# Other order of the seven products of a two-by-two block product in a decoder layer's feed-forward stages

## The chip, the cores and the metric

One core of one Trainium2 chip runs the whole kernel. The metric is the device time of one execution in microseconds (us). Its engines are TensorE (matmuls), VectorE, ScalarE and GpSimd (POOL) for element-wise work, and SyncE (SP), whose queue issues the weight loads. Each engine takes the instructions of its own queue in order; semaphores order them between engines.

## The reference

One layer of a decoder for 512 prompt tokens and 8 x 4 sample tokens, 544 columns in all; x is 544 x 1024, the hidden size of the feed-forward stages is 2816:

```
x = x + 0.5 * swiglu(rmsnorm(x, g1), wg1, wu1, wd1)      # feed-forward 1
h = rmsnorm(x, g2) @ w_in ; conv group and sparse attention group -> y
x = x + y @ w_out                                        # the middle stage
x = x + 0.5 * swiglu(rmsnorm(x, g3), wg2, wu2, wd2)      # feed-forward 2
swiglu(x, wg, wu, wd) = (silu(x @ wg) * (x @ wu)) @ wd
```

Everything is float32. The change touches only x @ wg and x @ wu of the two feed-forward stages.

## The kernel before

Activations lie transposed: 128 channels on the partitions, 544 token columns beside them, 8 chunks of channels. To keep float32 precision with TensorE's faster format, each operand is split into a high part (`whi`, rounded by ScalarE) and a low part (`wlo`, the rest, by VectorE), and a product is three matmuls: high by high, high by low, low by high.

A feed-forward stage runs over blocks of hidden chunks of 128 (`BLOCKS`, line 30): (0, 6), (6, 14), (14, 22) in the first, (0, 8), (8, 16), (16, 22) in the second. A block computes its hidden chunks and then multiplies them by their rows of `wd` (`Y`, lines 487 to 511), a stretch of 384 matmuls or less in which VectorE has little to do. The first six chunks of stage 1 and the first four of stage 2 are computed plainly (`G` and `U` at L195). All others go in pairs of chunks through `hidden` (line 415): 17 pairs, each a unit G (gate) and a unit U (up), 34 units in five stretches of 4, 4, 2, 4 and 3 pairs.

A unit (`unit`, line 362) is a two-by-two block product by Strassen's scheme in Winograd's form. The left side is the weight, in four quarters: a11 and a12 (halves of the inner dimension, first chunk of the pair), a21 and a22 (second chunk). The right side is the normed activation, halved by inner dimension and by columns. Seven products take the place of eight: three on raw quarters (a11, a12, a22) and four on sums s1 = a21 + a22, s2 = s1 - a11, s3 = a11 - a21, s4 = a12 - s2. Each is 12 matmuls of 272 columns (4 chunks by 3 split terms), so a unit is 84 matmuls. Counting from 0, the order of the products before is a11, s1, s2, a12, s3, s4, a22.

`factors` (line 268) prepares the left side of one unit. Two DMAs bring (a11, a12) and (a21, a22) into staging tiles `wst` (three in one pool and a fourth, `wst4`, so that two units' weights are staged). `parts` (line 282) splits: (a11, a12) together at line 293, 128 x 1024, from `wst`; (s1, s2) at line 298 and (s3, s4) at line 299, 128 x 1024 each, from `s`; a22 alone at line 300, 128 x 512, from `wst`. The sums are four POOL instructions (line 297) in tiles s12 and s34 of one buffer each. Split weights have few buffers: three slots `whi0` to `whi2`, one for each of the three pairs, and one pair of tiles for a22. So the split of a pair for the next unit can start only when both products of that pair in the running unit are done.

`right` (line 311) prepares the seven right-hand sides once a stage, in two halves of k0. Its splits are numbered 0 to 6 in the order in which they are written, and `self.rights` lists them for `unit`; the last is that of a22.

Products leave PSUM by ScalarE copies m1 and m5 (lines 375, 376) and VectorE additions into z, a tile of seven parts (lines 377, 379, 380, 381, 385), after which come silu (line 418), the product of gate and up (line 421) and the split of the hidden chunks hh, hl (lines 483, 484). PSUM tiles: f has two banks, s and t one each, w is two tiles of two banks.

The order on each engine's queue is not the order of the code: it is fixed before the run by the scheduler behind `TileContext`, which knows the dependencies and the buffers and gives each instruction its place. `unit` names the products in one order, and `factors` returns the left sides, and `self.rights` the right sides, in the same order.

Of the kernel before, what the change touches and what calls it, by code (L numbers as in the profile page):

```python
# [14 lines left out]
AF = mybir.ActivationFunctionType  # L15
# [6 lines left out]
HT = T // 2  # L22
# [99 lines left out]
class Trunk:  # L122
# [63 lines left out]
    def wmm(self, unit, parts, act, cuts=HALVES, which=(0, 1)):  # L186

        wh, wl = parts
        ah, al = act
        n = wh.shape[1]  # L190
        for k in range(n):
            for j, (a, b) in enumerate(((wh, ah), (wh, al), (wl, ah))):
                for i in which:
                    c0, c1 = cuts[i]
                    self.nc.tensor.matmul(unit[:, i, :c1 - c0], a[:, k, :], b[:, k, c0:c1],  # L195
                                          start=k == 0 and j == 0, stop=k == n - 1 and j == 2)
# [71 lines left out]
    def factors(self, srcs, nk):  # L268


        nc = self.nc
        st = []
        for load in srcs:
            self.staged += 1
            pool, tag = (self.fp, "wst4") if self.staged % 4 == 0 else (self.sp, "wst")
            t = pool.tile([128, 2 * nk * 128], F32, name="wst", tag=tag, bufs=1 if pool is self.fp else WB).rearrange("p (h k m) -> p h k m", h=2, k=nk)
            for dst, src in load(t):
                nc.sync.dma_start(dst, src)
            st.append(t)
        (a11, a12), (a21, a22) = [(t[:, 0], t[:, 1]) for t in st]  # L280

        def parts(src, n):
            if n == 1:
                ts = [self.fp.tile([128, nk * 128], F32R, name=nm, tag=nm + "4", bufs=1) for nm in ("whi", "wlo")]
            else:
                slot, self.slot = self.slot, (self.slot + 1) % 3
                ts = [self.sp.tile([128, n * nk * 128], F32R, name=nm, tag=f"{nm}{slot}", bufs=1) for nm in ("whi", "wlo")]
            hi, lo = (t.rearrange("p (h k m) -> p h k m", h=n, k=nk) for t in ts)
            nc.scalar.activation(hi, src, AF.Copy)  # L289
            nc.vector.tensor_sub(lo, src, hi.bitcast(F32))  # L290
            return [(hi[:, h], lo[:, h]) for h in range(n)]

        p11, p12 = parts(st[0], 2)
        s12, s34 = (self.fp.tile([128, 2, nk, 128], F32, name=n, tag=n, bufs=SB) for n in ("s12", "s34"))
        for dst, a, b, op in ((s12[:, 0], a21, a22, ALU.add), (s12[:, 1], s12[:, 0], a11, ALU.subtract),
                              (s34[:, 0], a11, a21, ALU.subtract), (s34[:, 1], a12, s12[:, 1], ALU.subtract)):
            nc.gpsimd.tensor_tensor(dst, a, b, op=op)  # L297
        p1, p2 = parts(s12, 2)
        p3, p4 = parts(s34, 2)
        p22, = parts(st[1][:, 1:2], 1)  # L300
        return p11, p1, p2, p12, p3, p4, p22

    def parts_of(self, u, k, hh, hl):

# [6 lines left out]
    def right(self, scale, place):  # L311


        nc, fp, n = self.nc, self.fp, KC // 2
        V, P = nc.vector, nc.gpsimd
        x3 = [fp.tile([128, 3, n, HT], F32R, name=nm, tag=nm, bufs=1) for nm in ("x3h", "x3l")]
        x4 = [self.xp.tile([128, 4, n, HT], F32R, name=nm, tag=nm, bufs=1) for nm in ("xh", "xl")]
        places = [(x3, 0), (x3, 1), (x3, 2), (x4, 0), (x4, 2), (x4, 1), (x4, 3)]
        self.rights = [[a[:, j] for a in t] for t, j in places]
        for k0 in range(0, n, 2):  # L320
            v, t3 = place(k0)

            def row(r):
                for k in range(2):
                    c, dst = r * n + k0 + k, v[r][:, k].rearrange("p c n -> p (c n)")
                    if r == 0 or self.alone:
                        V.scalar_tensor_tensor(dst, self.x[:, c, :], scale[:, c:c + 1], self.R, op0=ALU.mult, op1=ALU.mult)
                    else:
                        nc.scalar.activation(dst, self.x[:, c, :], AF.Copy, scale=scale[:, c:c + 1])
                        P.tensor_tensor(dst, dst, self.R, op=ALU.mult)  # L330

            def split(i, src):
                t, j = places[i]
                hi, lo = (a[:, j, k0:k0 + 2] for a in t)
                nc.scalar.activation(hi, src, AF.Copy)
                V.tensor_sub(lo, src, hi.bitcast(F32))

            (b11, b12), (b21, b22) = [[v[r][:, :, c] for c in range(2)] for r in range(2)]
            less = (V if self.alone else P).tensor_tensor
            row(0)  # L340
            split(0, b11)
            yield
            row(1)
            yield
            less(t3, b22, b12, op=ALU.subtract)
            V.tensor_sub(b12, b12, b11)
            split(1, b12)
            yield
            less(b11, b22, b12, op=ALU.subtract)
            split(2, b11)  # L350
            yield
            split(3, b21)
            yield
            split(4, t3)
            yield
            less(b21, b21, b11, op=ALU.subtract)
            split(5, b22)
            yield
            split(6, b21)
            yield  # L360

    def unit(self, name, left, right, nk, z):

        nc = self.nc
        V, EV = nc.vector, getattr(nc, EVICT)
        m1, m5 = (self.fp.tile([128, HT], F32, name=n, tag=n, bufs=ZB) for n in ("m1", "m5"))

        def product(n, out):
            (wh, wl), (bh, bl) = left[n], right[n]
            for k in range(nk):  # L370
                for j, (w, b) in enumerate(((wh, bh), (wh, bl), (wl, bh))):
                    nc.tensor.matmul(out, w[:, k, :], b[:, k, :], start=k == 0 and j == 0, stop=k == nk - 1 and j == 2)  # L372
            return out

        nc.scalar.activation(m1, product(0, self.funit(name)[:, :HT]), AF.Copy)  # L375
        nc.scalar.activation(m5, product(1, self.funit(name)[:, :HT]), AF.Copy)
        V.tensor_add(z[:, 0], product(2, self.sunit(name)[:, :HT]), m1)
        p = product(3, self.tunit(name)[:, :HT])
        V.tensor_add(z[:, 3], p, m1)
        V.tensor_add(z[:, 2], product(4, self.funit(name)[:, :HT]), z[:, 0])  # L380
        EV.tensor_tensor(z[:, 1::5], z[:, 0:3:2], m5[:, None, :].to_broadcast([128, 2, HT]), op=ALU.add)
        w = self.wunit(name)
        product(5, w[:, 0, :HT])
        product(6, w[:, 1, :HT])
        V.tensor_add(z[:, 4:6], w[:, :, :HT], z[:, 1:3])

    def ffn(self, wg, wu, wd, scale, done, late=False):
# [155 lines left out]
    def begin_units(self):  # L543

        nc, tc, i = self.nc, self.tc, self.i
        with tc.high_priority(offset=FIRST):
# [74 lines left out]
            def mms(unit, w, hf, order="01234567" * 2):  # L621

                c0, c1 = TILES[hf]
                seen = set()
                for n, ch in enumerate(order):
                    k = int(ch)
                    _, wh, wl = (x[:, k % x.shape[1]] for x in w[k * len(w) // KC])
                    todo = [(wl, self.xh)] if k in seen else [(wh, self.xh), (wh, self.xl)]
                    seen.add(k)
                    for a, b in todo:  # L630
                        pin(nc.tensor.matmul(unit[:, hf, :c1 - c0], a, b[:, k, c0:c1], start=n == 0 and b is self.xh, stop=n == 2 * KC - 1))
# [1068 lines left out]
```

## Time and profile before

| what | us |
|---|---|
| time, median of 3 runs | 1253.94 (1253.44 to 1253.94) |
| the profiled execution, its own time | 1253.65 |
| its span in the profile | 1251.9 |
| TensorE busy | 1192.6 (95%) |
| VectorE busy | 858.7 (69%) |
| ScalarE busy | 544.2 (43%) |
| POOL busy | 446.3 (36%) |
| L372, the units' matmuls | 2856 of the 9216 matmuls |

A busy share is a mean over stages with different limits. PE is TensorE's matmul row, DVE VectorE, ACT ScalarE. Matmuls are pipelined: each lasts 0.29 us in the profile, and the next starts 0.125 us after it.

### The profile page before, as it was taken

How to read it: one execution, taken by the hardware profiler on the slowest of the kernel's cores; microseconds unless marked ns; L12 is line 12 of the kernel's file. 1: busy time of each engine (PE TensorE's matmuls, PEld its weight loads, DVE VectorE, ACT ScalarE, POOL GpSimd, SP SyncE). 2: the span in 40 equal slices, each digit the busy share in tenths (PEclk: the TensorE clock that was granted, in tenths of full speed). 3: DMA queues.
4: the chain of work that ended last, by engine and by line, in shares of the span. 5: the costliest groups of instructions: out<-in, count | busy, mean ns of one | idle time of the engine just before them, and what ended most of it. 6: DMA issues, size and time to landing. Idle time of an engine off the chain costs nothing.

```text
span 1251.9 us, 22739 instructions
## 1 busy us (share of the span) xinstructions
PE 1192.6 (95%) x9216; PEld 1070.5 (86%) x9221; DVE 858.7 (69%) x1433; ACT 544.2 (43%) x830; POOL 446.3 (36%) x465
## 2 busy tenths in 40 slices
PE   8999999999999998899979999989989999999998
PEld 7999989999998747775667545779989999999998
DVE  6449998359965208999999753246997379845972
ACT  6224544134444455465534546335444134423432
POOL 2202651145302536665423222221650255204500
PEclk9999999999999998999998999999999999999999
DMA  8523224223331562245214544544223312432332
GB/s 239 140 68 105 73 86 134 86 69 90 94 104 59 168 199 85 65 139 169 66 58 142 163 135 140 164 136 135 77 60 110 110 55 86 123 93 71 95 86 75
DMA packets 184364, 136.08 MB, mean 109 GB/s; under 512 B 5706, under 2 KB 172434, under 8 KB 184260
## 3 DMA queue, kind: packets, MB, share of 16 engines
q1 hardware_dynamic: 171700, 91.62, 25.3%
q0 software_dynamic: 11904, 42.26, 10.5%
q8 instruction: 72, 1.18, 0.4%
q10 hardware_dynamic: 656, 0.76, 0.2%
q14 instruction: 32, 0.26, 0.1%
HBM read 131.66 MB, written 2.96 MB: 108 GB/s over the span
## 4 chain that ended last, share of the span: by engine, by line
PE 67%; DVE 22%; issue 5%; DMA 3%; ACT 2%; POOL 1%; DVEq 0%; ACTq 0%; POOLq 0%
PE Y L195 21%; PE U L372 10%; PE G L372 6%; DVE wlo L290 5%; PE Yo L134 3%; PE lg L134 3%; PE U L195 3%; PE nat L134 3%; PE KTp L138 3%; PE G L195 2%; DVE flip L1010 2%; DMA ckn<-in_cache_k,ik 1%; PE ssc L134 1%; DVE u L421 1%; PE O L134 1%
## 5 line engine op out<-in xcount | busy, mean ns | idle before, releaser
L297 POOL TENSOR_TENSOR s<-wst 128x512 f32<-128x512 f32 x68 | 98.2, 1448 | 363.7 <-DMA wst<-in_ffn_w_gate 209.0
L170 ACT ACTIVATE whi<-wst 128x1024 fp32r<-128x1024 f32 (+3 forms) x105 | 99.9, 957 | 203.9 <-PE Y L195 72.5
L195 PE MATMUL Y<-hl,whi 128*128 128x272 f32 (+2 forms) x704 | 147.8, 288 | 0.0
L195 PE MATMUL Y<-hh,whi 128*128 128x272 f32 (+2 forms) x704 | 147.6, 289 | 0.0
L195 PE MATMUL Y<-hh,wlo 128*128 128x272 f32 (+2 forms) x704 | 147.5, 288 | 0.0
L175 DVE TENSOR_TENSOR wlo<-wst,whi 128x1024 fp32r<-128x1024 f32 (+3 forms) x88 | 99.8, 1134 | 21.3 <-ACT whi L170 19.7
L195 PEld LDWEIGHTS Y<-hl,whi 128*128 128x128 f32 x704 | 111.5, 188 | 0.0
L195 PEld LDWEIGHTS Y<-hh,wlo 128*128 128x128 f32 x704 | 111.3, 188 | 0.0
L195 PEld LDWEIGHTS Y<-hh,whi 128*128 128x128 f32 x704 | 110.8, 188 | 0.0
L290 DVE TENSOR_TENSOR wlo<-wst,whi 128x1024 fp32r<-128x1024 f32 (+1 forms) x68 | 96.3, 1416 | 15.4 <-ACT whi L289 15.0
L509 DVE SCALAR_TENSOR_TENSOR x<-Y,x 128x544 f32<-128x544 f32 x46 | 33.2, 723 | 105.0 <-PE Y L195 105.0
L289 ACT ACTIVATE whi<-s 128x1024 fp32r<-128x1024 f32 x68 | 71.8, 1056 | 70.9 <-PE Y L195 29.8
L290 DVE TENSOR_TENSOR wlo<-s,whi 128x1024 fp32r<-128x1024 f32 x68 | 87.8, 1292 | 10.5 <-ACT whi L289 10.5
L372 PE MATMUL U<-xh,whi 128*128 128x272 f32 x272 | 78.5, 289 | 0.2 <-ACT m L375 0.2
L372 PE MATMUL G<-xh,wlo 128*128 128x272 f32 x272 | 78.4, 288 | 0.0
L372 PE MATMUL U<-xh,wlo 128*128 128x272 f32 x272 | 78.4, 288 | 0.0
L173 POOL TENSOR_TENSOR wlo<-wst,whi 128x1024 fp32r<-128x1024 f32 (+2 forms) x17 | 34.5, 2032 | 122.7 <-ACT whi L170 122.2
L372 PE MATMUL G<-xh,whi 128*128 128x272 f32 x272 | 78.3, 288 | 0.0
L372 PE MATMUL U<-xl,whi 128*128 128x272 f32 x272 | 78.1, 287 | 0.0
L372 PE MATMUL G<-xl,whi 128*128 128x272 f32 x272 | 78.1, 287 | 0.0
L289 ACT ACTIVATE whi<-wst 128x1024 fp32r<-128x1024 f32 (+1 forms) x68 | 57.2, 841 | 42.4 <-DMA wst<-in_ffn_w_gate 17.3
L372 PE MATMUL U<-x3h,wlo 128*128 128x272 f32 x204 | 61.4, 306 | 11.3 <-DVE wlo L290 11.3
(428 smaller groups left out, 3591.9 us busy)
## 6 DMA issues: line engine op xcount, KB each, us to landing
wst<-in_ffn_w_up SPq DMA_DIRECT2D x44, 512.0 KB, 4.3
wst<-in_ffn_w_gate SPq DMA_DIRECT2D x43, 512.0 KB, 3.8
wst<-in_ffn_w_down SPq DMA_DIRECT2D x32, 512.0 KB, 3.9
wst<-in_w_in SPq DMA_DIRECT2D x16, 512.0 KB, 3.7
wst<-in_ffn_w_down SPq DMA_DIRECT2D x16, 384.0 KB, 3.4
xin<-in_x_prompt SPq DMA_DIRECT2D x4, 512.0 KB
wst<-in_w_in SPq DMA_DIRECT2D x8, 256.0 KB, 4.9
wst<-in_w_out SPq DMA_DIRECT2D x8, 256.0 KB, 5.8
```

The costliest lines, as they stand in the source:

```text
L134: ins = self.nc.tensor.matmul(*args, **kw)
L138: ins = self.nc.tensor.transpose(*args)
L170: nc.scalar.activation(hi, st, AF.Copy)
L173: nc.gpsimd.tensor_tensor(lo, st, hi.bitcast(F32), op=ALU.subtract)
L175: nc.vector.tensor_sub(lo, st, hi.bitcast(F32))
L195: self.nc.tensor.matmul(unit[:, i, :c1 - c0], a[:, k, :], b[:, k, c0:c1], start=k == 0 and j == 0, stop=k == n - 1 and j == 2)
L289: nc.scalar.activation(hi, src, AF.Copy)
L290: nc.vector.tensor_sub(lo, src, hi.bitcast(F32))
L297: nc.gpsimd.tensor_tensor(dst, a, b, op=op)
L372: nc.tensor.matmul(out, w[:, k, :], b[:, k, :], start=k == 0 and j == 0, stop=k == nk - 1 and j == 2)
L509: nc.vector.scalar_tensor_tensor(xc, Y[:, :, :HT], 0.5, xc, op0=ALU.mult, op1=ALU.add)
L1010: V.tensor_scalar(junk, src, cand[:, k:k + 1], None, op0=ALU.is_ge, op1=ALU.add, accum_out=cnt[:, k:k + 1])
```

## The change

The seven products of a unit come in the order a11, a12, a22, s1, s2, s3, s4. `factors` returns the left sides in this order, `self.rights` lists the right sides to match, and `unit` takes each product's PSUM tile and eviction along: the product of a12 goes to t and is evicted with m1 as the second product, that of a22 goes to the second half of w, which is taken at that point, that of s1 gives m5, and that of s4 fills the first half of w as the last product. The splits, the sums and the loads are written in the same order as before.

```
-        return p11, p1, p2, p12, p3, p4, p22
+        return p11, p12, p22, p1, p2, p3, p4
...
-        self.rights = [[a[:, j] for a in t] for t, j in places]
+        self.rights = [[a[:, j] for a in places[i][0]] for i, j in ((i, places[i][1]) for i in (0, 3, 6, 1, 2, 4, 5))]
...
         nc.scalar.activation(m1, product(0, self.funit(name)[:, :HT]), AF.Copy)
-        nc.scalar.activation(m5, product(1, self.funit(name)[:, :HT]), AF.Copy)
-        V.tensor_add(z[:, 0], product(2, self.sunit(name)[:, :HT]), m1)
-        p = product(3, self.tunit(name)[:, :HT])
-        V.tensor_add(z[:, 3], p, m1)
-        V.tensor_add(z[:, 2], product(4, self.funit(name)[:, :HT]), z[:, 0])
+        V.tensor_add(z[:, 3], product(1, self.tunit(name)[:, :HT]), m1)
+        w = self.wunit(name)
+        product(2, w[:, 1, :HT])
+        nc.scalar.activation(m5, product(3, self.funit(name)[:, :HT]), AF.Copy)
+        V.tensor_add(z[:, 0], product(4, self.sunit(name)[:, :HT]), m1)
+        V.tensor_add(z[:, 2], product(5, self.funit(name)[:, :HT]), z[:, 0])
         EV.tensor_tensor(z[:, 1::5], z[:, 0:3:2], m5[:, None, :].to_broadcast([128, 2, HT]), op=ALU.add)
-        w = self.wunit(name)
-        product(5, w[:, 0, :HT])
-        product(6, w[:, 1, :HT])
+        product(6, w[:, 0, :HT])
         V.tensor_add(z[:, 4:6], w[:, :, :HT], z[:, 1:3])
```

## Rows read from the trace of the kernel before

**Rows 1.** The page, part 4: shares of the chain that ended last, by engine.
```profile
PE 67%; DVE 22%; issue 5%; DMA 3%; ACT 2%; POOL 1%; DVEq 0%; ACTq 0%; POOLq 0%
```
**Rows 2.** Waits of TensorE: waiter, releaser, us in total, times, longest.
```profile
PE U L372 <- DVE wlo L290: 11.3, 11, 2.0
...
PE gc L134 <- DVE yc L1193: 5.0, 1, 5.0
```
**Rows 3.** Busy times by window (PE, PEld, DVE, ACT, POOL, clock): two units; a pair.
```profile
1005.52:1026.59 21.07, 21.07 (x170) 21.07 (x169) 16.02 (x18) 10.54 (x13) 11.81 (x8) 1.00 0.20 59
1032.95:1056.23 23.28, 22.71 (x181) 22.49 (x180) 21.47 (x21) 10.69 (x15) 12.48 (x8) 1.00 0.31 90
```
**Rows 4.** The five stretches of units, windows of L372 alone: PE, PEld, clock.
```profile
124.52:214.04 89.52, 86.51 (x668) 85.49 (x668) 0.98 0.32 93
262.23:351.05 88.82, 86.59 (x672) 85.86 (x672) 0.98 0.29 83
909.31:957.49 48.18, 44.40 (x336) 43.69 (x336) 0.96 0.26 77
1005.52:1094.02 88.50, 85.73 (x672) 84.58 (x672) 1.00 0.31 89
1142.05:1207.25 65.20, 64.05 (x504) 63.33 (x504) 1.00 0.26 75
```
**Rows 5.** Window behind a stall, all engines; clock is the third number from the end.
```profile
181.95:185.83 3.88, 3.88 (x18) 3.88 (x19) 3.85 (x5) 0.40 (x1) 2.08 (x2) 0.56 0.46 135
```
**Rows 6.** Timeline of TensorE: first matmuls of three units, and a stall.
```profile
1026.59 0.29 PE L372 MATMUL G<-x3h,whi 128*128 128x272 f32 x1
...
1037.12 0.29 PE L372 MATMUL U<-x3h,whi 128*128 128x272 f32 x1
...
1038.98 0.39 PE L372 MATMUL U<-x3h,wlo 128*128 128x272 f32 x1 [0.57 <-DVE wlo L290]
...
1048.52 0.29 PE L372 MATMUL G<-x3h,whi 128*128 128x272 f32 x1
```
**Rows 7.** Timeline of VectorE: one split of a raw pair, two of a22.
```profile
1036.69 2.23 DVE L290 TENSOR_TENSOR wlo<-wst,whi 128x1024 fp32r<-128x1024 f32 x1
...
1042.35 1.37 DVE L290 TENSOR_TENSOR wlo<-wst,whi 128x512 fp32r<-128x512 f32 x1
...
1053.00 1.36 DVE L290 TENSOR_TENSOR wlo<-wst,whi 128x512 fp32r<-128x512 f32 x1
```
**Rows 8.** Timeline of ScalarE: splits of s1/s2 and of a11/a12.
```profile
1033.87 1.04 ACT L289 ACTIVATE whi<-s 128x1024 fp32r<-128x1024 f32 x1
1034.82 1.04 ACT L289 ACTIVATE whi<-wst 128x1024 fp32r<-128x1024 f32 x1
```
**Rows 9.** All splits of L290: ns at least, median, at most; first and last start.
```profile
L290 DVE TENSOR_TENSOR wlo<-wst,whi x68: 681/1356/2312, 114.5 to 1200.5; 128x512 fp32r<-128x512 f32 x34, 128x1024 fp32r<-128x1024 f32 x34
L290 DVE TENSOR_TENSOR wlo<-s,whi x68: 1207/1218/2320, 123.8 to 1198.7; 128x1024 fp32r<-128x1024 f32 x68
```
**Rows 10.** Waits of VectorE from 1005.52 to 1094.02.
```profile
DVE wlo L290 <- ACT whi L289: 2.8, 5, 0.8
...
DVE hl L484 <- ACT hh L483: 1.8, 3, 0.6
DVE u L377 <- ACT m L375: 1.2, 3, 0.9
```
**Rows 11.** Timeline of VectorE: the last right-hand split of stage 1.
```profile
127.96 1.19 DVE L336 TENSOR_TENSOR xl<-u,xh 128x544 fp32r<-128x544 f32 x1
```
**Rows 12.** Timeline of TensorE: a stall in the first unit of stage 2.
```profile
912.63 0.39 PE L372 MATMUL G<-x3h,wlo 128*128 128x272 f32 x1 [1.41 <-DVE wlo L290]
```
**Rows 13.** Timeline of POOL: a sum beside the raw pair's split.
```profile
1036.56 1.28 POOL L297 TENSOR_TENSOR s<-wst 128x512 f32<-128x512 f32 x1 [4.33 <-DVE wlo L290]
```
**Rows 14.** Timeline of ScalarE: splits for the first unit of the fourth stretch.
```profile
987.60 0.63 ACT L289 ACTIVATE whi<-wst 128x512 fp32r<-128x512 f32 x1 [5.06 <-DMA wst<-in_ffn_w_gate]
...
993.48 1.06 ACT L289 ACTIVATE whi<-wst 128x1024 fp32r<-128x1024 f32 x1 [4.29 <-PE Y L195]
```

## The prediction, made before the changed kernel ran

> **What bounds the kernel now.** The chain of waits is read first: two thirds of it is TensorE and 22% VectorE [rows 1], so the question is where VectorE stands in TensorE's way. TensorE's list of waits answers it: its longest entry is the unit's matmuls (L372, on U) waiting for the low part of a weight split (`wlo`, L290), 11 times [rows 2]. The five stretches in which the 34 units run give the price. Two units without a stall (168 matmuls) take 21.07 us, 0.1254 us a matmul [rows 3]. Against that the stretches lose 89.52 - 668 x 0.1254 = 5.75, 88.82 - 84.27 = 4.55, 48.18 - 42.13 = 6.05, 88.50 - 84.27 = 4.23 and 65.20 - 63.20 = 2.00 us [rows 4]: 22.6 us together, the most that any order of the products can win here. Part of it is clock: after the longest stall the granted clock is 0.56 on average for 3.9 us, mostly the lower level of 1.2 GHz instead of 2.4 [rows 5], and the three stretches with a clock below 1.00 each have one such fall [rows 4]; it is inside the 22.6 us.
>
> The timeline shows the stall itself. The unit G starts at 1026.59, U at 1037.12; U's matmul with `wlo` waits until 1038.98, because VectorE finished the split of the raw quarters a11, a12 at 1036.69 + 2.23 = 1038.92 [rows 6, 7]. That split comes late for two reasons. It may start only when the unit before has used up the same pair of buffers, and a12 is used by product 3, so 4 x 12 x 0.1254 = 6.0 us after that unit's start; and the queues of ScalarE and VectorE are behind by then. VectorE is close to its limit: a pair of units takes it 23.28 us, 21.47 busy [rows 3], against 21.07 that TensorE needs.
>
> **The change part by part.** No instruction is added or dropped: 84 matmuls a unit, the same four splits, sums and evictions. What moves is the time at which a buffer is given back and the time at which its next content is needed. One product is 12 x 0.1254 = 1.50 us; a split takes ScalarE 1.04 [rows 8] and VectorE 1.22 (a single quarter 0.68) [rows 9] at best, 2.23 [rows 7] where POOL is in the way. Times are from the start of a unit, and the third matmul of a product is the first that wants `wlo` (0.25 us in).
>
> Raw pair a11, a12: given back after product 3 (6.0), done at 6.0 + 1.04 + 1.22 = 8.3 at best, wanted at 10.53 + 0.25 = 10.8: 2.5 us to spare before. Now given back after product 1 (3.0), done at 5.3, wanted at 10.8: 5.5 us. Pair s1, s2: given back after product 2, wanted at product 1 of the next unit; now after product 4 and at product 3: 5 products either way, 5.5 us to spare. Pair s3, s4: from (5, 4) to (6, 5), 5.5 us again. Single quarter a22: from (6, 6) to (2, 2), 6 products either way. So the narrowest of the four, the one in [rows 6], gets 3.0 us more, and no other gets less. The splits' order in the queues should become a11/a12, a22, s1/s2, s3/s4, in the order in which their buffers come free.
>
> Evictions: the two products with m1 as second input end with products 1 and 4 now, m5 is read after product 5 as before after product 4, and the last eviction (L385 of before) still follows the last product. The two-bank tile w is taken at product 2 instead of 5; there are two, one for G and one for U, so it is taken back a whole unit after its eviction, and the cost is nothing while that eviction lags by less than 9 products, 13 us. If that cover went, TensorE would wait at product 2. The bank of f that z[:, 2] empties is wanted 4 products later (6.0 us) instead of 3. The weight DMAs wait for the staging tile, whose last reader was the split of a22, ended at 1043.72 [rows 7]; that reader moves forward, so the loads on SP's queue start earlier, never later. POOL's sums still follow the splits of the sums before them.
>
> VectorE decides whether the 3.0 us last. It must not only start earlier, it must keep up. Its idle time in the stretch of 88.50 us that ends at 1094.02, apart from waits for TensorE, is 2.8 + 1.8 + 1.2 = 5.8 us, all of it for ScalarE results queued behind something else (splits, hh, m1) [rows 10]. With the raw splits 3.0 us ahead of need, VectorE has another ready instruction at those places; without that idle time it ends 5.8 us sooner, more than the 4.23 us that TensorE loses in this stretch. Bounds: all of the loss goes (4.23) or none of the idle does (first rival). I take nearly all, 0.3 us left, here and in the three stretches like it.
>
> Two stretches begin differently. In the first (from 124.52) the change asks for the last right-hand split at product 2 instead of 6: it is done at 127.96 + 1.19 = 129.15 [rows 11], and product 2 wants it after 20 + 7 matmuls, 124.52 + 27 x 0.1254 = 127.9. That costs up to 1.3 us, or nothing if another product's matmuls are put ahead in the queue; I take 1.3. In the third the first unit stalls in product 1 for the split of s1, 1.41 us [rows 12]; s1 becomes product 3, wanted 3.0 us later, so that stall goes. VectorE has much to catch up there, and I leave 1.0 us.
>
> Left over: 1.3 + 1.0 + 4 x 0.3, where the first stretch is counted for both, 3.5 us. Gain 22.6 - 3.5 = 19.1 us. Against the profiled execution's own 1253.65 that is 1234.6; the median of the runs is 0.29 above it, so 1234.9, taken as 1235.
>
> The queues are laid out anew for the whole program, so in the middle stage between the two feed-forward stages neighbours may change places. The trace of before can't show that. The largest single wait of TensorE there is 5.0 us [rows 2]; I bound it by 5 us either way and take none.
>
> The Trainium skill (SBUF, "Who interferes with whom") says that a VectorE instruction with two SBUF inputs and a GpSimd instruction that reads SBUF exclude each other for the whole instruction. The trace agrees: the 2.23 us split overlaps a POOL sum of 1.28 us and is 1.01 us longer than the 1.22 of one alone [rows 7, 9, 13]. By that rule the two engines' time on the port should be added up, which is the first rival.
>
> **Rivals.** *VectorE keeps its pace.* On POOL a pair of units needs 8 sums x 1.28 = 10.2 us [rows 13]; on VectorE, of instructions with two SBUF inputs, 6 x 1.22 + 2 x 0.68 for splits, four element-wise ones of 544 columns (estimate 0.68, as 512 take) and one of 1088 (estimate 1.22): 12.6 us [rows 9]. If these exclude each other throughout, a pair takes 22.9 us, near the 23.28 measured [rows 3], and no order shortens it. Then the change gives each stretch 3.0 us of slack once and nothing more: 4 x 3.0 + 2.0 = 14.0 us, 1253.65 - 14.0 + 0.29 = 1239.9. For it: the two numbers are close. Against: VectorE idles 5.8 us in that stretch although it is late [rows 10], and instruction overheads are in the 1.28 and 1.22 but need not hold the port.
>
> *The single quarter is split last.* The code still writes the split of a22 behind the three pairs, while its product is now the third. If ScalarE and VectorE take them in that order, `wlo` of a22 ends as in before, 1043.72 and 1053.00 + 1.36 = 1054.36, which is 6.6 and 5.8 us after the units' starts at 1037.12 and 1048.52 [rows 6, 7]; it is wanted at 24 x 0.1254 + 0.25 = 3.3. TensorE would stand some 3.0 us in 29 units (the five that open a stretch have it early), 87 us, less the 22.6: slower, 1253.9 + 64 = 1318. It decides as soon as a22's split stands behind that of s3, s4. Against it: in before the queues already follow readiness, not code. The pair s1, s2 is split at 1033.87, ahead of a11, a12 at 1034.82 [rows 8], although it is written later; and ahead of the stretch at 1005 the single quarter goes first of all, at 987.60, although it is written last [rows 14].
>
> *The stall only changes its place* (the end of a stretch, where the last hidden part must be there before the down projection; the right-hand splits), and the time stays within 0.2%, 1253.9. For it: VectorE is nearly full. Against it: no row shows another wait close behind this one.
>
> **How the numbers follow.** Forecast, 19 us less: 0.65, its own range 1231 to 1238. VectorE keeps its pace, 1240: 0.21. No change: 0.05. The quarter split last, 1318: 0.07. The rest, 0.02, is the middle stage going against it. The range runs from all 22.6 us won (1231.3) with a little from the middle stage, 1230, to the first rival with its bad side of it, 1244. Faster by over 0.2% (2.5 us, about what a measurement of this kernel can tell from no change): 0.87; within: 0.05; slower: 0.08.
>
> **What would show it.** Right: TensorE's waits at the units' matmuls fall from 11 to three or fewer; four of the five stretches at 0.1254 us a matmul; the clock at 1.00 in all; on ScalarE the split of 512 columns directly behind that of the raw pair; VectorE's period for a pair below 22.3 us. First rival: a period of 23 us still, with stalls only in the last pair of a stretch. Second: waits of about 3 us in the third product of most units. Wrong altogether: units without stalls, and the time still above 1244, which would put the loss in the middle stage.

## The result, and the profile of the changed kernel

The changed kernel takes 1237.36 us (median of 5 runs, 1235.53 to 1240.16) against 1253.94 of the kernel before in the same series: ratio 0.9862, 95% interval 0.9848 to 0.9877. A second series (e11 below) gave 0.9872 (0.9856 to 0.9888). The forecast was 1235 with an own range of 1231 to 1238. A ratio here is formed from the single runs of its series; it is not quite the quotient of the two medians.

The page of the changed kernel, part 1 and part 4. TensorE's share of the chain was 67% and VectorE's 22% [rows 1]; now:

```profile
PE 1187.9 (96%) x9216; PEld 1068.6 (87%) x9221; DVE 858.7 (70%) x1433; ACT 546.3 (44%) x830; POOL 453.8 (37%) x465
...
PE 78%; DVE 15%; DMA 3%; issue 3%; ACT 1%; POOL 1%; ACTq 0%; DVEq 0%; POOLq 0%
```

TensorE's waits at the units' matmuls (waiter, releaser, us in total, times, longest). There were 11 behind the low part of a split [rows 2]; one is left, and one in the first stretch behind the last right-hand split:

```profile
PE U L372 <- DVE wlo L290: 2.3, 1, 2.3
PE G L372 <- DVE xl L336: 0.5, 1, 0.5
```

The five stretches, windows of L372 alone (length, PE, PEld, granted clock, DMA). Against [rows 4] they are 5.1, 4.7, 3.6, 4.4 and 2.2 us shorter, 20.0 us together. The second, fourth and fifth have no wait at all, and the clock is 1.00 in all five:

```profile
123.06:207.46 84.40, 83.89 (x668) 83.61 (x668) 1.00 0.34 94
255.65:339.77 84.12, 84.12 (x672) 84.06 (x672) 1.00 0.30 85
901.03:945.63 44.60, 42.32 (x336) 42.04 (x336) 1.00 0.27 76
993.74:1077.81 84.07, 84.07 (x672) 84.00 (x672) 1.00 0.33 92
1125.92:1188.97 63.05, 63.05 (x504) 62.99 (x504) 1.00 0.27 76
```

One pair of units in the fourth stretch, from one split of hidden values (`hl`) to the next, which is one period of VectorE (length, then busy PE, PEld, DVE, ACT, POOL). The pair of before had 23.28 us with 21.47 busy [rows 3], so VectorE idled 1.81 us; now it idles 0.65 us and is as busy as ever:

```profile
1022.27:1044.28 22.01, 22.01 (x178) 22.01 (x177) 21.36 (x22) 11.45 (x15) 13.36 (x9) 1.00 0.34 96
```

So VectorE's 22.01 still exceeds the 21.02 that TensorE needs for a pair (84.07 / 4). The timeline shows what that does: the starts of three units, and the splits of their raw pairs.

```profile
1025.27 0.28 PE L372 MATMUL U<-x3h,whi 128*128 128x272 f32 x1
...
1046.29 0.28 PE L372 MATMUL U<-x3h,whi 128*128 128x272 f32 x1
...
1067.30 0.28 PE L372 MATMUL U<-x3h,whi 128*128 128x272 f32 x1
```

```profile
1019.68 2.31 DVE L290 TENSOR_TENSOR wlo<-wst,whi 128x1024 fp32r<-128x1024 f32 x1
...
1041.69 2.32 DVE L290 TENSOR_TENSOR wlo<-wst,whi 128x1024 fp32r<-128x1024 f32 x1
...
1063.72 2.32 DVE L290 TENSOR_TENSOR wlo<-wst,whi 128x1024 fp32r<-128x1024 f32 x1
```

The splits end at 1021.99, 1044.01 and 1066.04; they are wanted 0.25 us into the unit, at 1025.52, 1046.54 and 1067.55. The margin shrinks from 3.5 to 2.5 to 1.5 us, a microsecond a pair, and the stretch ends before the margin is used up.

### The profile page after: what moved, and what is told of

Read it like the earlier page. It is cut to its first block, busy times and chain, and to the rows that moved or that the text cites. A ratio compares the mean times of both kernels' runs of the same rounds, so it can differ in the third digit from the quotient of the medians.

```text
span 1234.1 us, 22755 instructions
## 1 busy us (share of the span) xinstructions
PE 1187.9 (96%) x9216; PEld 1068.6 (87%) x9221; DVE 858.7 (70%) x1433; ACT 546.3 (44%) x830; POOL 453.8 (37%) x465
## 4 chain that ended last, share of the span: by engine, by line
PE 78%; DVE 15%; DMA 3%; issue 3%; ACT 1%; POOL 1%; ACTq 0%; DVEq 0%; POOLq 0%
PE Y L195 19%; PE U L372 14%; PE G L372 13%; PE Yo L134 4%; PE lg L134 3%; PE U L195 3%; PE nat L134 3%; PE KTp L138 3%; PE G L195 2%; DVE flip L1009 2%; DMA ckn<-in_cache_k,ik 1%; PE ssc L134 1%; PE O L134 1%; DVE wlo L175 1%; DVE xl L336 1%
## 5 line engine op out<-in xcount | busy, mean ns | idle before, releaser
L290 DVE TENSOR_TENSOR wlo<-wst,whi 128x1024 fp32r<-128x1024 f32 (+1 forms) x68 | 104.7, 1558 | 21.5 <-ACT whi L289 21.1
L290 DVE TENSOR_TENSOR wlo<-s,whi 128x1024 fp32r<-128x1024 f32 x68 | 88.0, 1294 | 4.4 <-ACT whi L289 4.4
L372 PE MATMUL G<-xl,whi 128*128 128x272 f32 x272 | 78.2, 287 | 0.5 <-DVE xl L336 0.5
L372 PE MATMUL G<-xh,wlo 128*128 128x272 f32 x272 | 78.3, 288 | 0.0
L372 PE MATMUL U<-xh,wlo 128*128 128x272 f32 x272 | 78.3, 288 | 0.0
L372 PE MATMUL G<-xh,whi 128*128 128x272 f32 x272 | 78.3, 288 | 0.0
L372 PE MATMUL U<-xh,whi 128*128 128x272 f32 x272 | 78.3, 288 | 0.0
L372 PE MATMUL U<-xl,whi 128*128 128x272 f32 x272 | 78.1, 287 | 0.0
L297 POOL TENSOR_TENSOR s<-wst,s 128x512 f32<-128x512 f32 x34 | 70.4, 2071 | 0.3
```

## The experiments

The table has, for each kernel, one pair in the fourth stretch as above, the five stretches together (windows of L372 alone, from the first matmul of a stretch to its last), and the time. For before the sum is 385.26 because its first matmuls start at 119.51, ahead of the window in [rows 4]. By the windows of [rows 4] and of the section above the sums are 380.2 and 360.2, which the expectations of e1 and e2 use; the expectation of e12 counts to the end of the last matmul, 0.8 us more. Each ratio is to the runs of before in the same series, whose median was 1254.39 for e1 to e4, 1254.43 for e5 to e8, 1254.13 for e9 to e11 and 1253.87 for e12.

| kernel | VectorE period = busy + idle | GpSimd busy | five stretches | time, ratio to before |
|---|---|---|---|---|
| before | 23.28 = 21.47 + 1.81 | 12.48 | 385.26 | 1253.94 |
| changed | 22.01 = 21.36 + 0.65 | 13.36 | 365.26 | 1237.36, 0.9862 |
| e1 a12 alone | 22.87 = 22.15 + 0.72 | 11.87 | 372.85 | 1243.39, 0.9918 (0.9899 to 0.9938) |
| e2 a22 alone | 24.17 = 22.09 + 2.08 | 12.42 | 393.45 | 1264.96, 1.0084 (1.0066 to 1.0102) |
| e3 a22 split last | 21.83 = 20.90 + 0.93 | 13.22 | 372.43 | 1241.77, 0.9902 (0.9878 to 0.9925) |
| e4 two buffers | 23.20 = 22.52 + 0.68 | 11.87 | 387.62 | 1253.93, 0.9992 (0.9980 to 1.0004) |
| e5 more VectorE work | 23.35 = 22.66 + 0.69 | 13.36 | 375.77 | 1246.58, 0.9934 (0.9912 to 0.9955) |
| e7 sum on GpSimd | 23.17 = 20.53 + 2.64 | 17.10 | 377.69 | 1249.69, 0.9960 (0.9944 to 0.9975) |
| e8 thin sums | 21.05 = 16.64 + 4.41 | 5.34 | 362.46 | 1230.40, 0.9807 (0.9789 to 0.9824) |
| e9 sums from PSUM | 22.74 = 21.48 + 1.26 | 13.67 | 381.58 | 1249.48, 0.9963 (0.9949 to 0.9977) |
| e10 same, old order | 22.65 = 21.51 + 1.14 | 12.38 | 376.70 | 1246.79, 0.9941 (0.9927 to 0.9955) |
| e11 changed again | 22.04 = 21.39 + 0.65 | 13.38 | 365.32 | 1238.03, 0.9872 |
| e12 before again | 23.34 = 21.53 + 1.81 | 12.40 | 385.89 | 1255.10, 1.0009 (0.9988 to 1.0030) |

**e1: a12 alone.** Against the changed kernel:

```
-        return p11, p12, p22, p1, p2, p3, p4
+        return p11, p12, p1, p2, p3, p4, p22
```

with the right-hand sides and evictions in the same order.

> Only a12's product is moved (a11, a12, s1, s2, s3, s4, a22); a22's stays last. My theory: the gain comes from the raw pair's buffer, which is given back two products earlier, so this one move carries it: five stretches together about 360 us, as in the changed kernel (360.2), no wait for the raw pair's low part in the steady units, 1235 to 1240 us. The wait of 0.5 us in the first stretch for the last right-hand split goes too, because that product is the last again. Rival: a22's early place carries part of it: then the stretches take some 370 us and the time is near 1245.

The result, 1243.39 us, lies between the two: it is about 60% of the gain, so my theory gave too much to this move. Its pair, as the row shown for the changed kernel:

```profile
1028.43:1051.30 22.87, 22.87 (x186) 22.87 (x185) 22.15 (x23) 10.90 (x15) 11.87 (x8) 1.00 0.32 93
```

VectorE's idle goes as in the changed kernel (0.72). But it is busy 0.8 us longer than with a22 moved too (22.15 against 21.36), and GpSimd 1.5 less (11.87 against 13.36): I read this as the time that the two spend waiting for each other, of which more falls on VectorE; no run tests that reading by itself. a22's early place carried the rest of the gain.

**e2: a22 alone.** `return p11, p1, p2, p12, p22, p3, p4`, and the rest accordingly.

> Only a22's product is moved (a11, s1, s2, a12, a22, s3, s4); a12's stays fourth. My theory: the raw pair is given back as late as before, so the stalls of about 2 us a pair remain: five stretches 377 to 383 us (380.2 before), the PE's waits for the raw low part are back, VectorE's period for a pair near 23.3, 1250 to 1257 us. Rival (any order with a22 off the last place helps, because its split leaves VectorE's crowd at the unit's end): 1245 or less.

This is a loss, 10.6 us against the 1254.39 of its series. VectorE idles 2.08 us a pair, where before it was 1.81: with a12 fourth the raw pair still comes back late. TensorE's waits in this kernel:

```profile
PE U L372 <- DVE wlo L290: 8.7, 9, 2.0
PE U L372 <- DVE s L381: 4.4, 9, 0.5
PE G L372 <- DVE u L381: 3.7, 7, 0.5
PE G L372 <- DVE wlo L290: 1.7, 2, 1.4
```

The second and third are new: the product s3 is sixth now instead of fifth, and its bank of f is wanted again by s1 of the next unit, with two products between in place of three. 0.5 us in sixteen units is the price of that place, 8.1 us in all, and the stretches are 8.2 us longer than before (393.45 against 385.26).

**e4: the order of before, with a buffer of its own for a12.**

```
...
-        p11, p12 = parts(st[0], 2)
+        p11, = parts(st[0][:, 0:1], 1, None)
+        p12, = parts(st[0][:, 1:2], 1, "a12")
...
```

The lines not shown give `parts` the name of the buffer and move m1 and m5 to two buffers that lie idle.

> The order of before, but a11 and a12 are split one by one, a12 into buffers of its own (m1 and m5 move to two buffers that lie idle, to make room). If the late give-back of the raw pair's buffer is the cause, most of the stalls go with no product moved: a11's buffer is free after the first product, a12's has six products to its next use; the price is one more VectorE instruction a unit (two of 512 columns at 0.68 to 1.36 us in place of one of 1024 at 1.23 to 2.3). Stretches 360 to 366 us, 1236 to 1243 us. If the order itself matters (what TensorE finds ready first), the stalls stay and the time is within 3 us of 1254.

The time is the rival's, but not for its reason. The raw low part makes TensorE wait only once, 0.9 us, and VectorE's idle falls from 1.81 to 0.68, as the theory has it. Its busy time rises by 1.05, because two instructions stand in place of one (a unit's splits of raw quarters are three of 512 columns, 1.20 us each on average, where before has one of 1024 columns at 1.60 and one of 512 at 1.23), and the backlog then shows at the next narrow place, a bank of PSUM that L381 empties:

```profile
PE U L373 <- DVE s L381: 11.0, 7, 2.8
PE U L373 <- ACT m L376: 1.3, 1, 1.3
PE G L373 <- DVE wlo L290: 0.9, 1, 0.9
```

So the late give-back explains VectorE's idle time, and it is not by itself what the stretches lose by: what counts here is VectorE's whole period, 23.20 us, nearly that of before. The period does not fix the loss alone either, as e3 and e5 show.

**e3: the second rival made true.** The splits of s3, s4 and of a22 are kept in the order of the code on ScalarE and VectorE (`pin` is taken for these two alone).

```
...
-            nc.scalar.activation(hi, src, AF.Copy)
-            nc.vector.tensor_sub(lo, src, hi.bitcast(F32))
+            pin(nc.scalar.activation(hi, src, AF.Copy))
+            pin(nc.vector.tensor_sub(lo, src, hi.bitcast(F32)))
...
```

> The changed kernel, but on ScalarE and VectorE the split of a22 is kept behind that of s3 and s4, as my second rival had it. That rival gives about 3.0 us a unit over 29 units: near 1318 us. I now expect less: the low part of s3, s4 ends 5.4 us into the unit that uses it in the changed kernel, a22's then 0.7 to 1.4 us behind it, that is 6 to 7 us into the unit where code order wants it at 3.25; TensorE's own queue is laid out anew with ten of a22's matmuls behind those of s1 or s2, which covers most of it. So between 0 and 1.5 us a unit, 1240 to 1280 us, with waits of PE in the a22 product.

The time is 1241.77 us, 4 to 5 us over the changed kernel, where the rival's price was 80. TensorE's waits for `wlo` are 5.3 + 1.3 us in the whole program, at most 1.0 each. In that kernel's queue two matmuls of a22 stand inside the product of s1 and the other ten behind most of s2 or s3. VectorE's period is the shortest of all with full sums, 21.83, so this place of the split is even the better one for VectorE. Yet the five stretches take 372.43 us, 7.2 more than in the changed kernel, so a shorter period alone does not shorten the stretches: here TensorE waits for `wlo` 6.6 us in all, in the changed kernel 2.3.

**e5: VectorE has more to do.** In the changed kernel the subtraction for a22 is made twice.

```
             nc.vector.tensor_sub(lo, src, hi.bitcast(F32))
+            if n == 1:
+                nc.vector.tensor_sub(lo, src, hi.bitcast(F32))
```

> The changed kernel, with VectorE's subtraction of a22's low part (128x512) made twice. The four runs before this one suggest a rule: VectorE sets the pace of a pair of units, and a stretch loses (its pairs) x (VectorE's period - 21.05) - about 5 us that stand in buffers at its start. By it the changed kernel (22.0 a pair) has next to nothing over, and an added 0.7 to 1.8 us a unit (alone, and beside GpSimd) makes the period 23.4 to 25.5: 4 to 12 us lost in each stretch of eight units, 1251 to 1280 us. Rival, my prediction's account (the raw pair's late give-back was the cause, and it is gone): the added work fits in VectorE's idle time, and the time stays at 1235 to 1241 us.

Neither came true: the time is 1246.58 us. The added 1.3 us a pair makes the period 23.35, as long as that of before, so VectorE's idle did not take it up, against the prediction's account. But a stretch of eight units loses 2.6 us (86.70 against 84.07), not 4 to 12: the new order has 4 x (23.35 - 21.02) - 2.6 = 6.7 us in hand, the old one at the same period 4 x (23.28 - 21.02) - 4.4 = 4.6. By this run the change did two things: a shorter period, and some 2 us more in hand in such a stretch. The second is not small: with VectorE's period as long as in before the five stretches still take 375.77 us, 9.5 less than before, about half of the change's 20. It is near the 3.0 us of slack once a stretch that the first rival allowed; that this slack is the reason is not shown, and e7, in the new order too, has only 4.4 us in hand in that stretch (granted clock 0.98) and 5.9 in the second.

**e6: a stretch of 14 units.** In the changed kernel, with the rows of hh and the down sums fitted to it (those lines are not shown):

```
...
-BLOCKS = [[(0, 6), (6, 14), (14, 22)], [(0, 8), (8, 16), (16, 22)]]
+BLOCKS = [[(0, 6), (6, 14), (14, 22)], [(0, 8), (8, 22)]]
...
```

> The changed kernel with the second network's last two stretches (8 and 6 units) made one of 14. It leaves out one round of down sums, takes 8 of the last 14 chunks into the other, and overwrites six rows of the hidden activations, so its whole time says nothing. By the rule (0.97 us lost on VectorE a pair, some 5 us in hand) the long stretch has no wait in its first ten units, then waits that sum to 1 to 3 us in the last four: 148 to 151 us for 1176 matmuls (147.5 at 0.1254). Rival (VectorE falls into TensorE's step once the buffers are in step): no wait at all, 147.5 us.

It went the way of the rule that e5's expectation states: no wait in the first nine units, then small ones. Here are the stretch, and two of the four waits in it that the timeline names, of 0.26 and 0.18 us, each of which comes twice:

```profile
993.63:1143.00 149.37, 148.46 (x1176) 147.37 (x1176) 1.00 0.32 89
```

```profile
1096.67 0.39 PE L372 MATMUL U<-xh,wlo 128*128 128x272 f32 x1 [0.26 <-DVE wlo L290]
...
1114.89 0.37 PE L372 MATMUL U<-x3h,whi 128*128 128x272 f32 x1 [0.18 <-DVE s L381]
```

149.4 is 1.9 us over 147.5; the four named waits make 0.9 of it, and for the rest the timeline names no wait. VectorE's period stays at 22.0 to the end of the stretch. The changed kernel's stretches are free of waits because they end in time, not because VectorE keeps up.

**e8: thin sums in the kernel before.** GpSimd's sums read and write 128 of 512 columns.

```
...
-        s12, s34 = (self.fp.tile([128, 2, nk, 128], F32, name=n, tag=n, bufs=SB) for n in ("s12", "s34"))
+        s12, s34 = (self.fp.tile([128, 2, nk, 128], F32, name=n, tag=n, bufs=SB)[:, :, :1] for n in ("s12", "s34"))
...
```

> The kernel before, with GpSimd's four sums of a unit cut to 128 of their 512 columns (the splits of the sums read those columns four times, so the values are not those of the products). The order, the buffers and the raw pair's give-back are as before. If VectorE's pace, lengthened beside GpSimd, is what the stretches lose by, its period falls from 23.28 to 21.3 or less and the waits go without any product moved: five stretches 360 to 366 us, 1234 to 1242 us. Rival (the raw pair's late give-back alone): the waits for the raw low part stay, stretches 375 us or more, 1247 to 1255 us.

The result is clear: TensorE has no wait at a unit's matmul in the whole program, in the old order and with the old buffers, and the time is below the changed kernel's. The pair, and (second fence) the eviction of 544 columns with both inputs in SBUF, with its least, median and greatest ns; the third fence has that instruction in the kernel before, from which e8 is made; the fourth has it, and one with an input in PSUM, in the changed kernel:

```profile
1018.10:1039.15 21.05, 21.05 (x170) 21.05 (x169) 16.64 (x23) 11.12 (x15) 5.34 (x8) 1.00 0.35 102
```

```profile
L383 DVE TENSOR_TENSOR s<-s,m x17: 724/725/728, 132.2 to 1176.0; 128x544 f32<-128x544 f32 x17
```

```profile
L381 DVE TENSOR_TENSOR s<-s,m x17: 724/1341/1356, 135.4 to 1198.1; 128x544 f32<-128x544 f32 x17
```

```profile
L382 DVE TENSOR_TENSOR s<-s,m x17: 724/1618/1627, 134.9 to 1181.0; 128x544 f32<-128x544 f32 x17
...
L384 DVE TENSOR_TENSOR s<-G,s x17: 724/724/726, 136.6 to 1181.8; 128x544 f32<-128x544 f32 x17
```

The same work of VectorE takes 16.64 us a pair beside thin sums and 21.47 beside full ones: 4.8 us of its "busy" is waiting for GpSimd inside its instructions. The thin sums also end sooner, but that is hardly what helps: in the stretches of before ScalarE waited for a weight sum three times only, in the first units of the first stretch and of the third, and VectorE never. L384, with one input in PSUM, takes 724 ns whatever GpSimd does. This is the rule that the prediction weighed (the Trainium skill, SBUF, "Who interferes with whom"), which also says that a VectorE instruction with at most one SBUF input, outside the two-port modes, stays out of it; the two rows agree.

**e7 and e9: less of that work on VectorE, in the changed kernel.** e7 sends the sum at L382 to GpSimd (`EVICT = "gpsimd"`). e9 keeps it on VectorE but reads PSUM (`m` holds m1 and the sum of m1 and the product s1, and `twice(p)` reads p twice over; their definitions are not shown):

```
...
-        nc.scalar.activation(m5, product(3, self.funit(name)[:, :HT]), AF.Copy)
-        V.tensor_add(z[:, 0], product(4, self.sunit(name)[:, :HT]), m1)
-        V.tensor_add(z[:, 2], product(5, self.funit(name)[:, :HT]), z[:, 0])
-        EV.tensor_tensor(z[:, 1::5], z[:, 0:3:2], m5[:, None, :].to_broadcast([128, 2, HT]), op=ALU.add)
+        V.tensor_add(m[:, 1], product(3, self.funit(name)[:, :HT]), m[:, 0])
+        V.tensor_add(z[:, 0:2], twice(product(4, self.sunit(name)[:, :HT])), m)
+        V.tensor_add(z[:, 2::4], twice(product(5, self.funit(name)[:, :HT])), z[:, 0:2])
...
```

> The changed kernel with one sum of each unit (544 columns, 1.62 us on VectorE) moved to GpSimd: 3.24 us a pair off VectorE. By the rule, if VectorE's own work sets the pace, its margins no longer shrink, the third stretch's 2.3 us wait goes, and the time is 1232 to 1238 us. Rival (VectorE is slowed by GpSimd, whose busy time rises from 13.4 to 17 or 18 us a pair): VectorE's period stays at 22 or rises, and the sums for the next unit come later: 1238 to 1250 us.

> The changed kernel with one sum of each unit rewritten so that VectorE reads it from PSUM: in place of ScalarE's copy of the s1 product, two sums of 272 columns (0.43 us each) and one of 544 in SBUF (1.62 us beside GpSimd, 0.72 alone), VectorE makes one of 272 (0.43) and two of 544 with one operand in PSUM (0.72 each, a form that the traces show at one length whatever GpSimd does). That takes 0.6 us a unit, 1.2 us a pair, off VectorE. Theory (two-SBUF-operand work beside GpSimd sets VectorE's pace): the period falls from 22.0 to TensorE's 21.05, the margins no longer shrink, the third stretch's wait of 2.3 us shrinks by about 1: 1233 to 1237 us, 0 to 3 us under the changed kernel of the same call. Rival: the period stays at 22 since GpSimd's sums only spread out; same time as the changed kernel.

e7 went the rival's way: 3.24 us a pair were taken from VectorE, its busy time fell by 0.83, and its period rose by 1.16. e9 missed on both sides: it is 11 us slower than the changed kernel. Its busy time did not fall at all (21.48); the collisions went to other instructions, the two products with `s` behind the last sum taking 2.44 us where the changed kernel's take 0.99 and 0.71:

```profile
1050.27 2.44 DVE L422 TENSOR_TENSOR u<-u,s 128x544 f32<-128x544 f32 x2
```

And the product s1, which ScalarE used to copy out at once, now holds its bank until VectorE's queue comes to it; these waits are the largest of TensorE's in e9's units:

```profile
PE U L375 <- DVE m L382: 13.7, 9, 3.4
```

**e10: e9's rewriting in the order of before.**

> The same rewriting in the kernel before, with its order of products. Theory: the period falls from 23.28 by 1.2 or more, to 22.1 or less, so a stretch of eight units loses 4 x 1.0 - 5, that is nothing: nearly all of the change's gain with no product moved, five stretches 361 to 368 us, 1236 to 1243 us. Rival (the raw pair's late give-back makes the stall by itself): the waits for the raw low part stay, 1249 us or more.

This came out half-way. The period of the table's pair falls by 0.63, not 1.2 or more, again because the busy time stays at 21.5, and the first two stretches are like it; only from the next pair of the fourth stretch on is it 22.0, with 20.9 busy. The time is 7 us better instead of 11 to 18. The rival's sign is there too, though its time is not: the waits for the raw low part stay, and are shorter.

```profile
PE U L375 <- DVE wlo L290: 9.1, 12, 1.4
```

A shorter period does help the old order without moving a product. The rule's "about 5 us in hand" is rough: by it 4.0 here, 3.6 in e9, 6.7 in e5, and 1.6 in e3.

**e11 and e12: both kernels again.**

> The changed kernel once more, unaltered, for a second profile beside the same runs of before. If the 3 us that the middle stage gave back belong to the change, the middle stage is again near 561.3 us; if they are spread from run to run (the identical queues of the long-stretch kernel took 559.7), it lies anywhere in 558 to 563. The time is 1235 to 1240 us.

> The kernel before once more, unaltered, for a second profile. The five stretches of the changed kernel were 366.06 and 366.12 us in its two profiles, 20 us under those of before (386.06), but the medians differ by 16 to 17; the middle stage was 558.1 us in the one profile of before and 559.7 to 561.4 in three with the changed kernel's queues. If the middle stage only scatters, this profile's lies anywhere in 558 to 563 and the time goes with it, and the stretches are again within 1 us of 386. If the 3 us belong to the change, the middle stage is again within 1 us of 558. If it is the stretches of before that vary (the clock's falls behind long waits), they are 1 us or more away from 386.

The stretches repeat to 0.1 us (changed) and 0.6 us (before), 20 us apart. The middle stage does not. Windows from the last unit of stage 1 to the first of stage 2: the changed kernel, e11, e12, each in its own fence.

```profile
339.77:901.03 561.26, 524.68 (x3931) 408.00 (x3935) 368.30 (x884) 272.52 (x469) 216.88 (x305) 0.98 0.40 123
```

```profile
339.89:901.46 561.57, 527.69 (x3931) 409.86 (x3935) 365.76 (x884) 272.87 (x469) 214.92 (x305) 0.97 0.40 123
```

```profile
351.60:912.11 560.51, 524.50 (x3936) 405.99 (x3935) 365.65 (x883) 271.67 (x468) 215.77 (x305) 0.98 0.40 123
```

The first profile of before had 558.3; e6, with the changed kernel's queues up to there, 559.9. Means of 559.4 and 560.9, each set scattered by about 2: that the change costs 1.5 us there is possible and not shown.

## Why the prediction held, step by step

- **What can be won, 22.6 us, and 0.1254 us a matmul.** Held: three of five stretches run at that pace or up to 0.0003 below it (the sign asked for four), and 20.0 of the 22.6 us went.
- **The raw pair's 3.0 us.** The step is right about the buffer: with a12 second (changed, e1) or with a buffer of its own (e4) VectorE's idle falls from 1.8 to 0.7 us a pair. It is not the whole cause. e4 shows that this idle can go and the stalls stay, and e1 that some 40% of the gain came with a22, which I had counted as even ("6 products either way").
- **"VectorE must keep up".** I took it that without idle time it would. It doesn't: 22.0 against 21.0 us a pair. The forecast came out because 4 pairs x 1.0 us is less than what the stretch has in hand, as e6 shows by making the stretch longer. The prediction has no term for what a stretch has in hand, so in this step the number held by luck: the stretches are short.
- **First rival, "VectorE keeps its pace".** It was right that GpSimd's sums set VectorE's pace (e8), and wrong that no order changes it: with full sums the orders tried gave 21.83 to 24.17 us. Its slack once a stretch may be part of the gain (e5).
- **Second rival.** Its order did not come about: ScalarE takes the 512-column split directly behind the raw pair's in U's turn, as one group (the x2 of the row below), and behind one `hh` in G's. Its price was wrong by a factor of nearly 20 (e3), since TensorE's queue is laid out anew too; in the order of matmuls that it took for granted the rival was not run.

```profile
1030.28 1.56 ACT L289 ACTIVATE whi<-wst 128x1024 fp32r<-128x1024 f32 x2
```

- **What is left over, 3.5 us.** 2.6 us were left, but the parts differ. The first stretch lost 0.6 instead of 1.6: the right-hand split ends 4.63 us into the stretch, as computed, but 32 matmuls stand ahead of the one that wants it, not 27; the third lost 2.5 instead of 1.0, in the wait of its second unit below; the other three nothing instead of 0.9.

```profile
914.24 0.40 PE L372 MATMUL U<-x3h,wlo 128*128 128x272 f32 x1 [2.28 <-DVE wlo L290]
```

- **The middle stage, taken as 0.** In the two profiled executions the middle stage is 3.0 us longer with the change, and with 1.5 us won ahead of the first stretch and 0.5 lost in the tail 20.0 becomes 17.8 (1253.65 - 1235.88). By e11 and e12 about half of the 3.0 is scatter. The second pair of profiled executions (1256.43 and 1237.9) is 18.5 us apart, the medians 16 to 17; that difference lies inside the scatter of single executions (1250.88 to 1257.32 for before in one series of 17), and what of it belongs to the middle stage stays open.

## What to carry to other kernels

Read an engine that paces a loop as period = busy + idle, and then ask how much of the busy time is itself waiting: the same instruction at 0.72 and 1.62 us in one trace says so. Moving work to where its inputs come free early removes the idle; it does not make the engine fast enough, and how long the loop runs decides whether that shows. An edit that shortens one instruction of such an engine can lengthen another by as much, and a result that a less busy engine used to take out of PSUM should stay with that engine.

## What was not expected

- The clock's falls cost next to nothing here. In the first profile of before three stretches had a granted clock below 1.00 [rows 4]; in e12 every stretch shows 1.00, and they are as long: 88.56 us at 1.00 against 88.82 at 0.98 (the second) and 47.93 at 1.00 against 48.18 at 0.96 (the third), while the first, at 1.00, is even 1.0 us longer than before's at 0.98. It fits that VectorE sets the pace there, so that a slower TensorE only uses up time in which it would have waited.
- VectorE and GpSimd together are busy 33.9 to 35.2 us a pair in before, changed, e1 to e4, e9 and e10 (the table's two columns added); the order seems to change mainly which of them does the waiting, which these sums suggest and no run isolates.
